# Linear attention taken four heads at a time, with its instructions regrouped and half of its weight-sum transfers moved

## The chip, the cores and the metric

The kernel runs on one core of a Trainium2 chip. The metric is the device time of one launch, in microseconds (us). The kernel before takes 1200.89 us, the median of three runs (1200.57 to 1201.19).

## What is computed

One transformer-like layer on x (1024 tokens by 1024 channels), in float32. Three mixers share one input projection, then an output projection and a squared-ReLU MLP of width 4096 follow:

```
h = rms_norm(x, ln1_g);  z = h @ w_in
y_conv = short_conv(...)            # 256 channels
y_diff = diff_attention(...)        # 4 heads, q and k 2 x 64, v 128
y_gla  = gla(g_q, g_k, g_v, g_g, ...)   # 4 heads of 64, chunks of 64 tokens
x = x + concat(y_conv, y_diff, y_gla) @ w_out
x = x + square(relu(rms_norm(x, ln2_g) @ w_mlp1)) @ w_mlp2
```

The change is in `gla`, the gated linear attention. For each chunk of 64 tokens and each head it needs three products (scores of the chunk with itself, those scores times v, and the queries times the state carried from the chunks before):

```
att     = where(causal, einsum('bcthd,bcshd->bchts', q_in, k_in), 0)
o_intra = einsum('bchts,bcshe->bcthe', att, vf)
o_inter = einsum('bcthd,bchde->bcthe', q_in, s_prev)
o = rms_norm(o_intra + o_inter, norm_g) * silu(g_out)
```

## The kernel before

**Products.** Large products keep float32 precision by splitting each operand into a high and a low part; `mm3` (L157 to L160) issues three matmuls for each piece: L158, L159, L160. A projection tile (`gemm_b`, L180) is 128 tokens by 256 columns of `w_in`: 8 pieces of the 1024 channels, so 24 matmuls, into one of three PSUM banks named `ps_mm`. The small products of linear attention are single float32 matmuls; each appears in the trace as two passes, each with a weight load (PEld) and a matmul (PE).

**Linear attention.** The four heads lie in two pairs (`pr`); within a pair, head `hh` has partitions 0 to 63 or 64 to 127 (`po = hh * 64`). `eb` holds the queries, `enb` the keys, `S` the states, `gv` the values. The loop before (L520 to L524) runs over 16 steps g: a token tile tt of 128 tokens and one hh, so two heads in each step. `gla_scores(g)` (L494) makes two matmuls that read 64 partitions and write 128 columns, then masks them into one of four tiles `att` (L496, VectorE). `gla_out(g)` adds up, for either pair, a full matmul `att` by `gv` (L506) and two matmuls of 64 partitions by 64 columns, `eb` by `S`, one for each chunk of the tile (L509), in one PSUM bank `ps_tr`; ScalarE copies the result out (L513) and squares it (L514), VectorE sums the squares (L515).

**What runs between.** The generator `steps01` yields one projection tile at each `next`: 8 tiles of q (`qraw`), 8 of k (`kraw`) and 8 of v (`dv`) for heads 0 and 1 of differential attention. The loop takes one tile in each step; the last 7 tiles run after it. Loads of `w_in` (L146, in `load_w`) go by SP's queue into two stage buffers `wst`; ScalarE and VectorE split them (L138, L139), one projection ahead of their use.

**Weight sums.** The MLP needs sums of blocks of its weights. They are made by transfers in device memory: POOL's queue copies a block (L118) and later adds another to it (L121). There are 64 such transfers of 1 MB each, in a fixed order: `w1s` (32), then `w2s` (32). `next_sum(when)` (L130 to L134) issues the next one: a tiny POOL copy `paced` (L132) waits for `when`, the transfer stands behind it in POOL's queue. In the kernel before they are paced by: 4 tiles of `kE`, 4 of `eb`, the 16 steps of the linear attention loop (on `ssg`), 8 query tiles in each of four attention heads (32, on `sso`), and 8 steps of the MLP.

A scheduler orders the instructions of each engine; the program sets what each depends on. Attention (`attention(0)` to `attention(3)`) follows the loop, with the other projections between. At the end of attention 3 the mixed outputs are stored to device memory (`ydram`, L218) and read back (L706) for the output projection; ScalarE and VectorE split them into `yTh` and `yTl`.

The order of a loop step, and its PSUM bank:

```
gla_scores(0)
for g in range(2 * NT):
    if g + 1 < 2 * NT:
        gla_scores(g + 1)
    next(steps01)
    gla_out(g)
```

Of the kernel before, what the change touches and what calls it, by code (L numbers as in the profile page):

```python
# [9 lines left out]
F32 = mybir.dt.float32  # L10
# [3 lines left out]
AF = mybir.ActivationFunctionType  # L14
ALU = mybir.AluOpType
AX = mybir.AxisListType
# [3 lines left out]
P = 128  # L20
T = 1024
D = 1024
NT = T // P
# [13 lines left out]
def hybrid_block(ctx, tc, x, ln1_g, w_in, conv_w, q_norm_g, k_norm_g, diff_lambda, diff_subln_g,  # L37
                 gla_alpha_w, gla_alpha_b, gla_norm_g, w_out, ln2_g, w_mlp1, w_mlp2, out):
    nc = tc.nc
# [19 lines left out]
    def ps_s():  # L59
        return psum.tile([P, 512], F32, name="ps_s", tag="s", bufs=2)  # L60

    def ps_tr():
        return psum.tile([P, 512], F32, name="ps_tr", tag="tr", bufs=2)
# [66 lines left out]
    def next_sum(when):  # L130

        g = nc.gpsimd.tensor_copy(paced, when)  # L132
        with tc.issue_after(g.ins):
            next(sum_steps)  # L134
# [6 lines left out]
    def load_w(w, c0, ncol):  # L141
        wb = []
        for kh in range(2):
            st = stage().rearrange("p (c n) -> p c n", c=4)
            wk = w[kh * 512:(kh + 1) * 512, :].rearrange("(c p) n -> p c n", p=P)
            nc.sync.dma_start(st, wk[:, :, c0:c0 + 256])  # L146
            hi = wpool.tile([P, 4, 272], F32R, name="whi", tag="hi", bufs=4)
            lo = wpool.tile([P, 4, 272], F32R, name="wlo", tag="lo", bufs=4)
            split(hi[:, :, 0:256], lo[:, :, 0:256], st)
            if ncol > 256:  # L150
                sx = c1.tile([P, 4, ncol - 256], F32, name="sx", tag="sx", bufs=2)
                nc.sync.dma_start(sx, wk[:, :, c0 + 256:c0 + ncol])
                split(hi[:, :, 256:ncol], lo[:, :, 256:ncol], sx)
            wb.append((hi, lo))
        return wb
# [10 lines left out]
    def gemm_a(wb, m0, mcols, act, th):  # L166
        ps = ps_mm()
        for kc in range(KC):
            hi, lo = wb[kc // 4]
            ah, al = act[th][kc // 4]  # L170
            mm3(ps[0:mcols, :], hi[:, kc % 4, m0:m0 + mcols], lo[:, kc % 4, m0:m0 + mcols],
                ah[:, kc % 4, :], al[:, kc % 4, :], kc == 0, kc == KC - 1)
        return ps

    def gemm_b(wb, act, tt, ncol=256, ks=tuple(range(KC))):
        ps = ps_mm()
        th, o = tt // 4, (tt % 4) * P
        for kc in ks:
            hi, lo = wb[kc // 4]
            ah, al = act[th][kc // 4]  # L180
            mm3(ps[:, 0:ncol], ah[:, kc % 4, o:o + P], al[:, kc % 4, o:o + P],
                hi[:, kc % 4, 0:ncol], lo[:, kc % 4, 0:ncol], kc == ks[0], kc == ks[-1])
        return ps
# [28 lines left out]
    gp = gla_cm.__enter__()  # L212

    def g4(nm):
        return gp.tile([P, 1024], F32, name=nm, tag="g4", bufs=8)
# [7 lines left out]
    def c4(nm):  # L223
        return cv.tile([P, T], F32, name=nm, tag="cz", bufs=3)
# [63 lines left out]
    gv = r1.tile([P, NT, 256], F32, name="gv", tag="v")  # L288
# [75 lines left out]
    eb = [g4("eb") for _ in range(2)]  # L364
    enb = [g4("enb") for _ in range(2)]
    dec = [c1.tile([P, 16], F32, name=f"dec{p}") for p in range(2)]
    for pr in range(2):
        for th in range(2):
            ps = ps_s()
            for i in range(4):  # L370
                tt = th * 4 + i
                c0 = (tt % 4) * 256 + pr * P
# [8 lines left out]
    for pr in range(2):  # L381
        for th in range(2):
            ts_ = slice(th * 512, (th + 1) * 512)
            ps = gemm_a(wb, pr * P, P, hT, th)
# [11 lines left out]
    S = [g4("S") for _ in range(2)]  # L396
    for pr in range(2):
        nc.gpsimd.memset(S[pr][:, 0:64], 0.0)
        kv = [ps_s(), ps_s()]
        for c in range(15):  # L400
            tt, po = c // 2, (c % 2) * 64
            for hh in range(2):
# [3 lines left out]
                                 start=True, stop=True)  # L406
# [9 lines left out]
    for pr in range(2):  # L416
        for th in range(2):
            ts_ = slice(th * 512, (th + 1) * 512)
            ps = gemm_a(wb, pr * P, P, hT, th)
# [8 lines left out]
        nc.vector.tensor_tensor(gv_, gv_, sg, op=ALU.mult)  # L428


    def qk_steps(c0, nm, got):
        wb = load_w(w_in, c0, 256)
        raw = r1.tile([P, NT, 256], F32, name=nm, tag="raw")
        got.append(raw)
        ss = stat.tile([P, 32], F32, name="ssqk", tag="ssqk", bufs=4)
        for tt in range(NT):
            ps = gemm_b(wb, hT, tt)
            nc.scalar.copy(raw[:, tt, :], ps[:, 0:256])
            sq = r1.tile([P, 256], F32, name="sqa", tag="sqa")
            nc.scalar.activation(sq, ps[:, 0:256], AF.Square)  # L440
            nc.vector.tensor_reduce(ss[:, tt * 4:tt * 4 + 4], sq.rearrange("p (h e) -> p h e", e=64),
                                    axis=AX.X, op=ALU.add)
            if tt % 4 == 3:
                th = tt // 4
                mq = stat.tile([P, 16], F32, name="mq", tag="mq")
                nc.vector.tensor_scalar(mq, ss[:, th * 16:th * 16 + 16], 1.0 / 64, EPS, op0=ALU.mult, op1=ALU.add)
                rq = rstd_of(mq, 16, "q16")
                for i in range(4):
                    rv = raw[:, th * 4 + i, :].rearrange("p (a e) -> p a e", e=64)
                    nc.vector.tensor_tensor(rv, rv, rq[:, i * 4:i * 4 + 4].unsqueeze(2).broadcast_to([P, 4, 64]),  # L450
                                            op=ALU.mult)
            yield

    def v_steps(pair, got):
        wb = load_w(w_in, C_DV + pair * 256, 256)
        v = r1.tile([P, NT, 256], F32, name="dv", tag="v")
        got.append(v)
        for tt in range(NT):
            ps = gemm_b(wb, hT, tt)
            nc.scalar.copy(v[:, tt, :], ps[:, 0:256])  # L460
            yield

    def run(steps):
        for _ in steps:
            pass

    def qk_raw(c0, nm):
        got = []
        run(qk_steps(c0, nm, got))
        return got[0]  # L470

    def v_proj(pair):
        got = []
        run(v_steps(pair, got))
        return got[0]

    qkv01 = []
    steps01 = chain(qk_steps(C_DQ, "qraw", qkv01), qk_steps(C_DK, "kraw", qkv01), v_steps(0, qkv01))


    attb = [gp.tile([P, 2, P], F32, name=f"att{i}") for i in range(4)]
    for a in attb:
        nc.gpsimd.memset(a, 0.0)
    og = [c4("og") for _ in range(2)]
    ssg = c1.tile([P, 32], F32, name="ssg")
    maskv = cum.bitcast(I32).unsqueeze(1).broadcast_to([P, 2, P])
    next(steps01)

    def gla_scores(g):
        tt, hh = g // 2, g % 2  # L490
        tsl, po = slice(tt * P, (tt + 1) * P), hh * 64
        ps = ps_s()
        for pr in range(2):
            nc.tensor.matmul(ps[:, pr * P:(pr + 1) * P], enb[pr][po:po + 64, tsl], eb[pr][po:po + 64, tsl],  # L494
                             start=True, stop=True)
        nc.vector.copy_predicated(attb[g % 4], maskv, ps[:, 0:256].rearrange("p (h t) -> p h t", h=2))  # L496

    def gla_out(g):
        tt, hh = g // 2, g % 2
        po, att = hh * 64, attb[g % 4]  # L500
        ov = og[tt // 4][:, (tt % 4) * 256:(tt % 4) * 256 + 256].rearrange("p (r h e) -> p r h e", r=2, h=2)
        po_ = ps_tr()
        for pr in range(2):
            os_ = slice(pr * 64, (pr + 1) * 64)
            h0 = pr * P + hh * 64
            nc.tensor.matmul(po_[:, os_], att[:, pr, :], gv[:, tt, h0:h0 + 64], start=True, stop=False)  # L506
            for i in range(2):
                c = tt * 2 + i
                nc.tensor.matmul(po_[i * 64:(i + 1) * 64, os_],  # L509
                                 eb[pr][po:po + 64, c * 64:(c + 1) * 64],  # L510
                                 S[pr][po:po + 64, c * 64:(c + 1) * 64], start=False, stop=True)
        sq = gp.tile([P, P], F32, name="sqg", tag="sqg", bufs=2)
        nc.scalar.copy(ov[:, :, hh, :], po_[:, 0:P].rearrange("p (r e) -> p r e", r=2))  # L513
        nc.scalar.activation(sq, po_[:, 0:P], AF.Square)  # L514
        nc.vector.tensor_reduce(ssg[:, tt * 4:tt * 4 + 4].rearrange("p (r h) -> p r h", r=2)[:, :, hh],  # L515
                                sq.rearrange("p (r e) -> p r e", r=2), axis=AX.X, op=ALU.add)
        next_sum(ssg[0:1, tt * 4 + hh:tt * 4 + hh + 1])

    gla_scores(0)
    for g in range(2 * NT):  # L520
        if g + 1 < 2 * NT:
            gla_scores(g + 1)
        next(steps01)
        gla_out(g)  # L524
    for th in range(2):
        mg = stat.tile([P, 16], F32, name="mg", tag="mg")
        nc.vector.tensor_scalar(mg, ssg[:, th * 16:th * 16 + 16], 1.0 / 64, EPS, op0=ALU.mult, op1=ALU.add)
# [1 line left out]
        ov = og[th].rearrange("p (a e) -> p a e", e=64)  # L529
# [132 lines left out]
    zs = r1.tile([P, 2, T], F32, name="zs", tag="v")  # L662
    wb = load_w(w_in, C_U, 256)
    for m in range(2):
        for th in range(2):
            ps = gemm_a(wb, m * P, P, hT, th)
            nc.scalar.copy(zs[:, m, th * 512:(th + 1) * 512], ps)
    attention(3, (q23, k23, v23), bias)
    wb = load_w(w_in, C_C, 256)
    accs = []  # L670
    for m in range(2):
        for th in range(2):
            ps = gemm_a(wb, m * P, P, hT, th)
# [36 lines left out]
    for m in range(2):  # L710
        for th in range(2):
            ps = gemm_a(wb, m * P, P, hT, th)
# [80 lines left out]
    for tt, nh in [(t, h) for h in range(2) for t in range(NB)] + [(t, h) for t in range(NB, NT) for h in range(2)]:  # L793
        if tt not in x1:
            x1_tile(tt)
        ps = gemm_o(tt, nh)
# [3 lines left out]
        if waiting:  # L800
            t = waiting.pop(0)
# [250 lines left out]
```

## Time and profile before

| | |
|---|---|
| median of three runs | 1200.89 us (1200.57 to 1201.19) |
| the profiled execution, its own time | 1198.36 us |
| its span, first to last instruction | 1196.7 us |
| TensorE (PE) matmul busy | 1175.5 us, 98% |
| PE weight loads (PEld) busy | 994.8 us, 83% |
| VectorE (DVE) / ScalarE (ACT) / POOL busy | 743.8 / 518.5 / 73.2 us |
| mean granted TensorE clock | 0.997 of full |

Times in the trace are us from the span's start. PE and PEld are two views of one engine: a weight load may run beside an earlier matmul, and the end of a matmul is modelled, so the starts of successive weight loads tell the pace. The linear attention loop lies at about 139 to 212 us, attention 0 to 3 at about 236 to 472 us, the output projection from there to about 570 us, then the MLP. In a row, `<-` behind a bracketed number names what ended the engine's idle time before the instruction.

### The profile page before, as it was taken

To read this page: it belongs to the slowest core of one execution; us is meant where nothing else is said; L and a number is where in the kernel's file an instruction comes from. 1 tells how busy PE (TensorE), PEld (TensorE's weight loads), DVE (VectorE), ACT (ScalarE), POOL (GpSimd) and SP (SyncE) were. 2 spreads that over 40 slices of the span, in tenths; PEclk is the share of its full clock that TensorE was granted. 3 is DMA by queue.
4 is the path that set the end of the run, shared out by engine and by line. 5 is a ranking of instruction groups with operands and counts; after the bars stand their busy time and mean duration, and the time that the engine had idled before them with its cause. 6 is when DMAs were issued, how large, how long until landed. Compare 5 with 4: busy or idle time off the path is not lost.

```text
span 1196.7 us, 16779 instructions
## 1 busy us (share of the span) xinstructions
PE 1175.5 (98%) x6423; PEld 994.8 (83%) x6423; DVE 743.8 (62%) x1334; ACT 518.5 (43%) x976; POOL 73.2 (6%) x159
## 2 busy tenths in 40 slices
PE   8999999999999998999999999999999999999998
PEld 6997899989997886788788888888888888888887
DVE  6535654386849695546877677667674654565553
ACT  5542133366647653423653434343433333333332
POOL 3001121010201111000000000000000000000000
PEclk9999999999999999999999999999999999999999
DMA  6124699758744979741566776777799985666000
GB/s 193 58 71 176 201 215 270 183 168 180 214 122 98 230 211 213 233 143 53 165 196 206 242 233 215 203 220 229 242 359 391 386 300 208 214 213 208 1 36 35
DMA packets 117074, 231.35 MB, mean 193 GB/s; under 512 B 7651, under 2 KB 49665, under 8 KB 113666
## 3 DMA queue, kind: packets, MB, share of 16 engines
q1 hardware_dynamic: 100290, 160.00, 39.3%
q0 software_dynamic: 14976, 67.14, 23.7%
q10 hardware_dynamic: 1728, 3.15, 0.7%
q8 instruction: 50, 0.82, 0.3%
q14 instruction: 30, 0.25, 0.1%
HBM read 189.37 MB, written 108.00 MB: 248 GB/s over the span
## 4 chain that ended last, share of the span: by engine, by line
PE 85%; DVE 5%; DMA 4%; ACT 4%; issue 1%; SPq 0%; POOL 0%; ACTq 0%; DVEq 0%; POOLq 0%
PE pso L158 8%; PE pso L160 8%; PE pso L159 8%; PE psp L159 8%; PE psp L160 8%; PE psp L158 8%; PE ps_mm L158 8%; PE ps_mm L160 7%; PE ps_mm L159 7%; PE ps_av L628 3%; PE ps_s L598 1%; PE ps_tr L620 1%; DMA wst<-in_w_out_dram 1%; PE ps_s L599 1%; DMA ydram<-yt 1%; DMA wst<-ydram 1%
## 5 line engine op out<-in xcount | busy, mean ns | idle before, releaser
L158 PE MATMUL pso<-o2l,o2h 128*128 128x512 f32 x448 | 174.3, 389 | 0.0
L159 PE MATMUL pso<-o2h 128*128 128x512 f32 x448 | 174.3, 389 | 0.0
L160 PE MATMUL pso<-o2h,o2l 128*128 128x512 f32 x448 | 174.3, 389 | 0.0
L139 DVE TENSOR_TENSOR o2l<-f,o2h 128x1024 fp32r<-128x1024 f32 x56 | 68.5, 1224 | 139.9 <-ACT o2h L138 139.9
L158 PE MATMUL ps_mm<-wlo,hTh 128*128 128x256 f32 (+1 forms) x512 | 148.2, 290 | 3.2 <-DVE wlo L139 2.5
L160 PE MATMUL ps_mm<-whi,hTl 128*128 128x256 f32 (+1 forms) x512 | 146.3, 286 | 0.0
L159 PE MATMUL ps_mm<-whi,hTh 128*128 128x256 f32 (+1 forms) x512 | 146.1, 285 | 0.0
L138 ACT CAST o2h<-f 128x1024 fp32r<-128x1024 f32 x56 | 59.0, 1053 | 191.7 <-PE pso L159 186.4
L158 PEld LDWEIGHTS ps_mm<-wlo,hTh 128*128 128x128 f32 x512 | 97.2, 190 | 7.3 <-ACT hTh L203 3.4
L160 PEld LDWEIGHTS pso<-o2h,o2l 128*128 128x128 f32 x448 | 84.1, 188 | 17.5
L159 PEld LDWEIGHTS pso<-o2h 128*128 128x128 f32 x448 | 84.1, 188 | 17.5
L158 PEld LDWEIGHTS pso<-o2l,o2h 128*128 128x128 f32 x448 | 84.1, 188 | 17.3
L160 PEld LDWEIGHTS ps_mm<-whi,hTl 128*128 128x128 f32 x512 | 97.3, 190 | 1.2 <-issue 0.7
L159 PEld LDWEIGHTS ps_mm<-whi,hTh 128*128 128x128 f32 x512 | 97.0, 189 | 1.2 <-issue 0.7
L138 ACT CAST w1h<-wst 128x1024 fp32r<-128x1024 f32 x56 | 59.1, 1055 | 85.6 <-PE psp L159 77.0
L886 DVE TENSOR_TENSOR s<-psp,s 128x512 f32<-128x512 f32 x96 | 64.6, 688 | 44.9 <-PE psp L160 40.3
L139 DVE TENSOR_TENSOR w1l<-wst,w1h 128x1024 fp32r<-128x1024 f32 x56 | 68.4, 1221 | 21.6 <-ACT w1h L138 21.5
L158 PE MATMUL ps_mm<-hTl,whi 128*128 128x512 f32 x160 | 65.2, 407 | 5.8 <-DVE yt L714 5.8
L139 DVE TENSOR_TENSOR o2l<-w,o2h 128x1024 fp32r<-128x1024 f32 x56 | 68.2, 1218 | 0.0
L159 PE MATMUL ps_mm<-hTh,whi 128*128 128x512 f32 x160 | 65.5, 409 | 0.0
L160 PE MATMUL ps_mm<-hTh,wlo 128*128 128x512 f32 x160 | 64.6, 404 | 0.0
L138 ACT CAST o2h<-w 128x1024 fp32r<-128x1024 f32 x56 | 58.9, 1052 | 2.8 <-PE psp L159 2.8
(309 smaller groups left out, 2457.5 us busy)
## 6 DMA issues: line engine op xcount, KB each, us to landing
f<-fdram SPq DMA_DIRECT2D x28, 1024.0 KB, 8.7
w1s<-in_w_mlp_dram POOLq DMA_DIRECT2D x24, 1024.0 KB, 9.5
w2s<-in_w_mlp_dram POOLq DMA_DIRECT2D x24, 1024.0 KB, 11.9
wst<-w1s SPq DMA_DIRECT2D x32, 512.0 KB, 4.2
w<-w2s SPq DMA_DIRECT2D x16, 1024.0 KB, 7.2
wst<-in_w_in_dram SPq DMA_DIRECT2D x26, 512.0 KB, 5.1
wst<-in_w_mlp_dram SPq DMA_DIRECT2D x24, 512.0 KB, 4.1
fdram<-s SPq DMA_DIRECT2D x48, 256.0 KB, 2.3
```

What stands on the lines that cost most here:

```text
L138: nc.scalar.copy(hi, src)
L139: return nc.vector.tensor_tensor(lo, src, hi.bitcast(F32), op=ALU.subtract)
L158: nc.tensor.matmul(ps, lh, rl, start=first, stop=False)
L159: nc.tensor.matmul(ps, lh, rh, start=False, stop=False)
L160: return nc.tensor.matmul(ps, ll, rh, start=False, stop=last)
L598: nc.tensor.matmul(ps[:, 0:w], qi, kll[c][:, j * 512:j * 512 + w], start=True, stop=False)
L599: nc.tensor.matmul(ps[:, 0:w], qi, khh[c][:, j * 512:j * 512 + w], start=False, stop=True)
L620: nc.tensor.transpose(tp[:, b * P:(b + 1) * P], pc[0][:, (b0 + b) * P:(b0 + b + 1) * P], ident)
L628: nc.tensor.matmul(av[:, 0:P], aT[:, b * P:(b + 1) * P], v[:, kb, hh * P:hh * P + P], start=(kb == 0), stop=(kb == i))
L886: nc.vector.tensor_tensor(dst, a_, b_, op=op)
```

## The change

The linear attention loop now runs over 8 token tiles, all four heads in each, with two projection tiles taken between. Matmuls that read partitions 0 to 63 and those that read 64 to 127 alternate and write different PSUM banks (`ps[0]`, `ps[1]`; `po_[0]`, `po_[1]`). The full matmuls of the tile (four) stand together, then the eight of 64 by 64, then the four score matmuls of the next tile. The loop issues 8 weight-sum transfers instead of 16; the other 8 are issued in projections after it: 2 in the v projection of heads 2 and 3, 4 in their q and k projections, 2 in the first convolution projection. The 64 transfers and their order stay.

```diff
-    def qk_steps(c0, nm, got):
+    def qk_steps(c0, nm, got, sums=False):
...
+                if sums:
+                    next_sum(rq[0:1, 0:1])
             yield
 
-    def v_steps(pair, got):
+    def v_steps(pair, got, sums=False):
...
+            if sums and tt % 4 == 3:
+                next_sum(v[0:1, tt, 0:1])
             yield
...
-        run(qk_steps(c0, nm, got))
+        run(qk_steps(c0, nm, got, True))
...
-        run(v_steps(pair, got))
+        run(v_steps(pair, got, True))
...
+    def gla_scores(tt):
+        tsl = slice(tt * P, (tt + 1) * P)
+        ps = [ps_s(), ps_s()]
         for pr in range(2):
+            for hh in range(2):
+                po = hh * 64
+                nc.tensor.matmul(ps[hh][:, pr * P:(pr + 1) * P], enb[pr][po:po + 64, tsl], eb[pr][po:po + 64, tsl],
+                                 start=True, stop=True)
+        for hh in range(2):
+            nc.vector.copy_predicated(attb[tt % 2 * 2 + hh], maskv, ps[hh][:, 0:256].rearrange("p (h t) -> p h t", h=2))
+
+    def gla_out(tt):
+        po_ = [ps_tr(), ps_tr()]
+        for hh in range(2):
+            for pr in range(2):
+                h0 = pr * P + hh * 64
+                nc.tensor.matmul(po_[hh][:, pr * 64:(pr + 1) * 64], attb[tt % 2 * 2 + hh][:, pr, :], gv[:, tt, h0:h0 + 64],
+                                 start=pr == 0, stop=False)
         for pr in range(2):
             for i in range(2):
                 c = tt * 2 + i
+                for hh in range(2):
+                    po = hh * 64
+                    nc.tensor.matmul(po_[hh][i * 64:(i + 1) * 64, pr * 64:(pr + 1) * 64],
+                                     eb[pr][po:po + 64, c * 64:(c + 1) * 64],
+                                     S[pr][po:po + 64, c * 64:(c + 1) * 64], start=False, stop=pr == 1)
...
+        next_sum(ssg[0:1, tt * 4:tt * 4 + 1])
...
     gla_scores(0)
-    for g in range(2 * NT):
-        if g + 1 < 2 * NT:
-            gla_scores(g + 1)
-        next(steps01)
-        gla_out(g)
+    for tt in range(NT):
+        for _ in range(2):
+            next(steps01)
+        gla_out(tt)
+        if tt + 1 < NT:
+            gla_scores(tt + 1)
...
             nc.scalar.copy(zs[:, m, th * 512:(th + 1) * 512], ps)
+        next_sum(zs[0:1, m, 512:513])
```

**TensorE, one step of the loop before** (g = 2; `att2` and the banks `ps_tr`, `ps_s` as named above, the numbers are those of buffers; the row behind is the next projection tile's first):

```order
L506 MATMUL ps_tr_1604<-gv_254,att2_1408 128x64
L509 MATMUL ps_tr_1604<-S_1164,eb_970 64x64 x2
L506 MATMUL ps_tr_1604<-gv_254,att2_1408 128x64
L509 MATMUL ps_tr_1604<-S_1165,eb_971 64x64 x2
L494 MATMUL ps_s_1617<-eb_970,enb_972 128x128
L494 MATMUL ps_s_1617<-eb_971,enb_973 128x128
L158 MATMUL ps_mm_1621<-wlo_1420,hTh_118 128x256
```

**TensorE, the tile tt = 1 now**, which is what the steps g = 2 and 3 were (the full matmuls are L510, two on each bank; those of 64 by 64 are L517; the scores L500):

```order
L510 MATMUL ps_tr_1631<-gv_254,att2_1408 128x64 x2
L510 MATMUL ps_tr_1632<-gv_254,att3_1409 128x64 x2
L517 MATMUL ps_tr_1631<-S_1164,eb_970 64x64
L517 MATMUL ps_tr_1632<-S_1164,eb_970 64x64
L517 MATMUL ps_tr_1631<-S_1164,eb_970 64x64
L517 MATMUL ps_tr_1632<-S_1164,eb_970 64x64
...
L500 MATMUL ps_s_1655<-eb_970,enb_972 128x128
L500 MATMUL ps_s_1656<-eb_970,enb_972 128x128
L500 MATMUL ps_s_1655<-eb_971,enb_973 128x128
L500 MATMUL ps_s_1656<-eb_971,enb_973 128x128
```

A step went from full to 64 by 64, back to full, to 64 by 64, and to the scores before the projection; a tile now goes through each form once, and successive matmuls of 64 partitions stand in different banks. Behind the loop, the order of the matmuls is as before.

**POOL's queue at the loop's end, before** (`w1s_100` is a sum that receives its second block, `w1s_101` the next one's copy; IOTA belongs to attention 0):

```order
L132 COPY paced<-ssg 1x1
L121 DMA w1s_100<-in_w_mlp_dram 128x2048
L547 IOTA bias 128x1024
L132 COPY paced<-ssg 1x1
L118 DMA w1s_101<-w1s_99 16x16384
L132 COPY paced<-ssg 1x1
L118 DMA w1s_101<-w1s_99 16x16384
```

and now:

```order
L132 COPY paced<-ssg 1x1
L121 DMA w1s_100<-in_w_mlp_dram 128x2048
L132 COPY paced<-sso 1x1
L118 DMA w1s_101<-w1s_99 16x16384
L132 COPY paced<-sso 1x1
L118 DMA w1s_101<-w1s_99 16x16384
```

The copies into `w1s_101` and all behind them now wait for `sso`, the query tiles of attention 0, instead of the loop; the order of the transfers is the same. SP's queue is unchanged row by row.

## Rows read from the trace of the kernel before

**Rows 1.** The page, part 1 (busy us, share, instructions) and part 4 (chain).

```profile
PE 1175.5 (98%) x6423; PEld 994.8 (83%) x6423; DVE 743.8 (62%) x1334; ACT 518.5 (43%) x976; POOL 73.2 (6%) x159
...
PE 85%; DVE 5%; DMA 4%; ACT 4%; issue 1%; SPq 0%; POOL 0%; ACTq 0%; DVEq 0%; POOLq 0%
```

**Rows 2.** Windows: busy us (instructions) by engine, granted clock, DMA share, GB/s.

```profile
139.57:211.59 72.02, 72.02 (x608) 65.63 (x607) 34.67 (x95) 22.18 (x73) 14.77 (x31) 1.00 0.93 222
...
405.00:427.00 22.00, 21.66 (x110) 16.63 (x109) 17.11 (x45) 14.78 (x33) 1.80 (x4) 1.00 1.01 219
427.00:443.00 16.00, 16.00 (x95) 13.49 (x94) 15.53 (x47) 9.70 (x29) 2.87 (x6) 1.00 0.80 263
443.00:472.50 29.50, 29.50 (x162) 24.00 (x160) 18.22 (x40) 10.81 (x27) 4.83 (x8) 1.00 1.01 202
...
478.37:484.00 5.63, 5.63 (x14) 4.43 (x15) 5.45 (x9) 4.00 (x7) 0.00 (x0) 0.51 0.58 181
```

**Rows 3.** Timeline of weight loads: start us, us covered, load, xcount; first, second, last step.

```profile
139.57 0.52 PEld L494 LDWEIGHTS ps_s<-eb,enb 64*128 64x128 f32 x4
140.20 0.19 PEld L158 LDWEIGHTS ps_mm<-wlo,hTh 128*128 128x128 f32 x1
...
144.57 0.19 PEld L160 LDWEIGHTS ps_mm<-whi,hTl 128*128 128x128 f32 x1
144.69 0.31 PEld L506 LDWEIGHTS ps_tr<-gv,att 128*128 128x128 f32 x2
145.07 0.19 PEld L509 LDWEIGHTS ps_tr<-S,eb 64*64 64x64 f32 x4
145.33 0.30 PEld L506 LDWEIGHTS ps_tr<-gv,att 128*128 128x128 f32 x2
145.69 0.20 PEld L509 LDWEIGHTS ps_tr<-S,eb 64*64 64x64 f32 x4
145.96 0.52 PEld L494 LDWEIGHTS ps_s<-eb,enb 64*128 64x128 f32 x4
146.59 0.19 PEld L158 LDWEIGHTS ps_mm<-wlo,hTh 128*128 128x128 f32 x1
...
210.33 0.31 PEld L506 LDWEIGHTS ps_tr<-gv,att 128*128 128x128 f32 x2
...
211.59 0.31 PEld L535 LDWEIGHTS ps_tr<-ident,og 128*128 128x128 f32 x3
```

**Rows 4.** Groups of the stretch 139.5 to 211.7 us: busy us, mean ns, idle before.

```profile
L506 PEld LDWEIGHTS ps_tr<-gv,att 128*128 128x128 f32 x64 | 9.7, 189 | 1.1
...
L494 PEld LDWEIGHTS ps_s<-eb,enb 64*128 64x128 f32 x64 | 8.3, 186 | 1.2
...
L509 PEld LDWEIGHTS ps_tr<-S,eb 64*64 64x64 f32 x128 | 6.2, 131 | 2.2
...
L513 ACT COPY og<-ps_tr 128x128 f32<-128x128 f32 x15 | 4.0, 265 | 9.1 <-PE ps_tr L509 9.1
```

**Rows 5.** Timeline of weight loads at the state products of one pair (L403).

```profile
131.29 1.42 PEld L403 LDWEIGHTS ps_s<-gv,kE 64*64 64x64 f32 x60 [0.25 <-issue]
```

**Rows 6.** Timeline of ScalarE: two splits' casts in the loop, then the stores behind it.

```profile
170.07 1.05 ACT L138 CAST whi<-wst 128x1024 fp32r<-128x1024 f32 x1
...
205.12 1.05 ACT L138 CAST whi<-wst 128x1024 fp32r<-128x1024 f32 x1 [1.80 <-PE ps_mm L160]
...
226.80 0.69 ACT L537 ACTIVATE yt<-ps_tr,cols 128x512 f32<-128x512 f32 x1 [2.64 <-DMA ydram<-yt]
```

**Rows 7.** Loads of `w_in` (L146) issued at 165 to 212 us, their landing.

```profile
DMA to landing us min/median/max: 17.7/19.1/25.9
```

**Rows 8.** Timeline of PE: the idle times at 228 and 478 us.

```profile
228.31 0.39 PE L158 MATMUL ps_mm<-wlo,hTh 128*128 128x256 f32 x1 [0.51 <-ACT dv L460]
...
478.37 0.80 PE L158 MATMUL ps_mm<-hTl,whi 128*128 128x512 f32 x1 [5.82 <-DVE yt L714]
```

**Rows 9.** Timeline of ScalarE: the wait for the outputs read back.

```profile
472.99 0.62 ACT L138 CAST yTh<-wst 128x512 fp32r<-128x512 f32 x1 [8.77 <-DMA wst<-ydram]
```

**Rows 10.** Uses of `w1s`: transfers, first and last start us.

```profile
L832 SPq DMA_DIRECT2D wst<-w1s x32: 359/371/386, 507.3 to 857.4; - x32
...
L121 POOL DMA_DIRECT2D w1s<-in_w_mlp_dram x16: 812/827/857, 144.0 to 279.4; - x16
```

More of the change, by code (lines that the diff above doesn't have):

```diff
@@ L487, in hybrid_block @@
     next(steps01)
[L489 to L492, printed above, removed]
+    def gla_scores(tt):
+        tsl = slice(tt * P, (tt + 1) * P)
+        ps = [ps_s(), ps_s()]
         for pr in range(2):
-            nc.tensor.matmul(ps[:, pr * P:(pr + 1) * P], enb[pr][po:po + 64, tsl], eb[pr][po:po + 64, tsl],
-                             start=True, stop=True)
-        nc.vector.copy_predicated(attb[g % 4], maskv, ps[:, 0:256].rearrange("p (h t) -> p h t", h=2))
@@ L498, in gla_out @@
[L498 to L502, printed above, removed]
+            for hh in range(2):
[4 more added lines that the diff above has]
+            nc.vector.copy_predicated(attb[tt % 2 * 2 + hh], maskv, ps[hh][:, 0:256].rearrange("p (h t) -> p h t", h=2))
@@ L503, in gla_out @@
+    def gla_out(tt):
[5 more added lines that the diff above has]
+                                 start=pr == 0, stop=False)
         for pr in range(2):
-            os_ = slice(pr * 64, (pr + 1) * 64)
-            h0 = pr * P + hh * 64
-            nc.tensor.matmul(po_[:, os_], att[:, pr, :], gv[:, tt, h0:h0 + 64], start=True, stop=False)
@@ L507, in gla_out @@
             for i in range(2):
                 c = tt * 2 + i
[L509 to L514, printed above, removed]
@@ L515, in gla_out @@
-        nc.vector.tensor_reduce(ssg[:, tt * 4:tt * 4 + 4].rearrange("p (r h) -> p r h", r=2)[:, :, hh],
-                                sq.rearrange("p (r e) -> p r e", r=2), axis=AX.X, op=ALU.add)
-        next_sum(ssg[0:1, tt * 4 + hh:tt * 4 + hh + 1])
-    gla_scores(0)
-    for g in range(2 * NT):
-        if g + 1 < 2 * NT:
-            gla_scores(g + 1)
-        next(steps01)
-        gla_out(g)
+                for hh in range(2):
[3 more added lines that the diff above has]
+                                     S[pr][po:po + 64, c * 64:(c + 1) * 64], start=False, stop=pr == 1)
@@ new lines, in gla_out @@
+        ov = og[tt // 4][:, (tt % 4) * 256:(tt % 4) * 256 + 256].rearrange("p (r h e) -> p r h e", r=2, h=2)
+        for hh in range(2):
+            sq = gp.tile([P, P], F32, name="sqg", tag="sqg", bufs=2)
+            nc.scalar.copy(ov[:, :, hh, :], po_[hh][:, 0:P].rearrange("p (r e) -> p r e", r=2))
+            nc.scalar.activation(sq, po_[hh][:, 0:P], AF.Square)
+            nc.vector.tensor_reduce(ssg[:, tt * 4:tt * 4 + 4].rearrange("p (r h) -> p r h", r=2)[:, :, hh],
+                                    sq.rearrange("p (r e) -> p r e", r=2), axis=AX.X, op=ALU.add)
```

## The prediction

> **What bounds the kernel now.** I read the page first: TensorE is busy 98% of the span and carries 85% of the chain that ended last [rows 1]. Then the windows: in the linear attention loop, 139.57 to 211.59 us, PE is busy for all of its 72.02 us, while VectorE needs 34.67 and ScalarE 22.18 [rows 2]. So a microsecond less of TensorE work there is a microsecond less of time, unless something behind it becomes late. The DMA share in the loop is 0.93: the memory queues are nearly full, but nothing waits for them there.
>
> Then the timeline of weight loads, since their starts give TensorE's pace [rows 3]. Between two projection matmuls it is 0.12 us (144.57 to 144.69). A loop step's small products start at 144.69 and the projection is back at 146.59: 1.90 us. Its parts, start to start:
> - full loads (L506), two: 144.69 to 145.07, 0.38 us
> - 64 by 64 (L509), four: 145.07 to 145.33, 0.26 us
> - both again: 145.33 to 145.96, 0.63 us
> - scores (L494), four: 145.96 to 146.59, 0.63 us
>
> The reader is to see two things. A pair of full loads covers 0.31 us, so the second starts 0.31 - 0.19 = 0.12 us after the first; yet the next form comes 0.26 us after that second load. Changing the form costs about 0.14 us more than a load in the same form. And the four 64 by 64 loads, each 131 ns [rows 4], cover only 0.19 us: the two of different columns run side by side, a second pass follows 0.06 us behind. The score loads, 186 ns each [rows 4], cover 0.52 us with four, so they follow each other at (0.52 - 0.19) / 3 = 0.11 us: they all stand on the same 64 partitions and take turns.
>
> **The change, part by part.** *Removed:* the small products of the loop before take 2 x 0.63 us (the first two score groups, such as 139.57 to 140.20), 14 steps of 1.90 us and 2 last steps of 1.26 us (such as 210.33 to 211.59) [rows 3]: 1.3 + 26.6 + 2.5 = 30.4 us.
>
> *Added:* per tile of four heads, no matmul more or less.
> - Eight full loads together: the first two and the change of form 0.38 us, six more at 0.11: 1.04 us.
> - Sixteen 64 by 64 loads, four on each quarter of the array. If the quarters run side by side, each has two passes more than in the row, at 0.06: 0.26 + 0.12 = 0.38 us.
> - Eight score loads, four on either half of the partitions. If the halves run side by side: 0.63 + 0.01 = 0.64 us.
>
> That is 2.06 us a tile, 1.42 without scores. Total: the first scores 1.3 us (still in two groups, as the order shows no alternation there), 8 x 1.42 = 11.4, 7 x 0.64 = 4.5: 17.1 us. **The loop gains 30.4 - 17.1 = 13.3 us.** The full matmuls and the changes of form are paid from rows; the running side by side of different partitions is the open term. The nearest row is the 60 loads of 64 by 64 for the state products: in pairs they would take 30 x 0.06 = 1.8 us, they took 1.42 [rows 5]; the order puts most matmuls of one half before those of the other. So halves do overlap where the order lets them. Bounds of the gain: with no overlap of halves, the quarters go in pairs (0.26 + 3 x 0.12 = 0.62 us) and the scores in turn (0.63 + 4 x 0.11 = 1.07): 2.73 a tile, 1.3 + 8 x 1.66 + 7 x 1.07 = 22.1 us in all, a gain of 8.3. With full overlap, 13.3. I take 13.3, since the row lies between and the new order alternates at every matmul.
>
> The Trainium skill, "TensorEngine Tiling (Array Packing)", section Key Properties, says that a change of tiling mode drains the engine and that tiles otherwise run independently; the trace agrees on the first with its 0.14 us a change, and by that rule alone, seven of ten changes saved in each of 8 tiles, an estimate would be 56 x 0.14 = 7.8 us.
>
> *New waits in the loop.* Each tile's masks, squares and copies now follow two projection tiles (2 x 24 x 0.12 = 5.7 us) instead of one; ScalarE and VectorE have well under half of the stretch to do [rows 2], and both `ps_tr` banks and both `ps_s` banks have those 5.7 us to come free. I cost this at nothing; without that cover a tile would wait for a copy out of PSUM, 0.27 us [rows 4], 2 us over 8 tiles. The w_in loads for the next projection but one are issued when the stage is split (170.07) and needed 35 us later (205.12) [rows 6]; they land in 17.7 to 25.9 us [rows 7]. The shorter loop leaves 8 steps of projection less 13.3 / 2: some 28 us, still above the worst row, and with half of the sum transfers in the way they land sooner.
>
> *Behind the loop.* The sums there held up a store: ScalarE waited for `ydram` (2.64 us at 226.80 [rows 6]) and PE lost 0.51 us to it [rows 8]. With 8 transfers fewer I take that 0.5 us as gained; bounds 0 and 0.5.
>
> *The moved sums.* Eight POOL copies and eight issues change their place in POOL's queue; behind them there stand only other sums, and SP's queue is untouched. `w1s` is first read at 507.3 us, its last sum was issued at 279.4 [rows 10] and comes some 40 us later now: 180 us to spare. By the end of attention 3, 56 transfers are issued as before, and its own eight are the same ones. But from the start of attention 2 to there go 18 transfers instead of 16, where the DMA share is 1.01 at 405 to 427 and 443 to 472 us [rows 2]. The stretch between them, 0.80, can take the two more (0.2 x 16 = 3.2 us free). Cost: none, with an upper bound among the rivals.
>
> **The sum:** 13.3 + 0.5 = 13.8 us. The profiled execution took 1198.36 us, so 1184.6; the median of the runs is 2.5 us above it, 1200.89, and the measured time should be **1187.1 us**.
>
> **The rivals.**
> *The halves do not overlap, or in part.* For: the score loads in the trace never alternate halves, so nothing shows it for that shape. Against: the 1.42 us of [rows 5]. Gain 8.3 + 0.5 at the least: 1192.1 us; half way, 1189.6. The Trainium skill, "TensorE: Matmul & The Clock Gate", Part 3, holds that matmuls start and end in program order, without reordering. Applied to passes, a matmul's second pass would hold back the next matmul's first, and the gain would fall between these two; the four L509 loads that cover 0.19 us speak against it here.
>
> *The stall at 472 us moves.* ScalarE waits 8.77 us for the outputs read back [rows 9], PE then 5.82 us [rows 8]; after that idle time the clock is granted at 0.51, the 1.2 GHz level, for 5.63 us [rows 2], half of which, 2.8 us, is lost. The change alters neither, but it shifts when they fall. Without the drop: 1184.3 us; with a drop of twice the length, 1189.9.
>
> *Slower.* At that same wait the two transfers more that cross the full queues could delay the read-back. PE idles one to one with it there. From 13.8 us of delay on, the gain is gone; the worst landing of a load in a crowded stretch was 25.9 us [rows 7], against a wait of 8.77 here: 17.1 us more, and the time would be 1187.1 + 17.1 = 1204.2 us. Against: the free 3.2 us before it, and the same eight transfers beside it.
>
> *Nothing changes* only if that delay comes to 11.4 to 16.2 us.
>
> **How the numbers follow.** The forecast has 0.68, the halves 0.14, the stall 0.11, slower 0.03, no change 0.03, and 0.01 for the rest. About 0.2% (2.4 us) is what a measurement here tells from no change. The first three all lie beyond it on the fast side: faster 0.94, same 0.03, slower 0.03. The range reaches from the stall without its drop and a read-back 1 us sooner, 1183.3, to the lower bound of the overlap, 1192.1, with 0.3 for the runs' own spread: 1183.0 to 1192.4 us.
>
> **What the profile will show.** Right: the loop lasts about 58.7 us instead of 72.0, PE busy throughout; a tile's small products take 2.06 us from the first L510 load to the projection; sixteen L517 loads cover about 0.3 us and eight L500 loads about 0.53; no idle PE at 228 less 13 us; the same 5.8 us stall after attention 3. Wrong: L500 loads at 0.11 us in one row after another (2.5 to 2.7 us a tile); PE idle in the loop on ScalarE or VectorE; a ScalarE wait on `ydram` well above 8.77 us.

## The result and the profile after

The changed kernel takes 1186.20 us (median of 4 runs, 1185.81 to 1186.57) against 1200.73 us (4 runs, 1199.83 to 1201.19) for the kernel before: ratio 0.9878, 95% interval 0.9866 to 0.9889, so 14.5 us faster. Its profiled execution took 1186.37 us, with a span of 1184.7.

The page of the changed kernel, parts 1 and 4, answers to [rows 1]:

```profile
PE 1161.1 (98%) x6423; PEld 986.0 (83%) x6423; DVE 743.8 (63%) x1334; ACT 517.8 (44%) x976; POOL 75.0 (6%) x159
...
PE 88%; DVE 5%; ACT 3%; DMA 2%; issue 1%; SPq 0%; POOL 0%; ACTq 0%; DVEq 0%; POOLq 0%
```

TensorE has the same 6423 matmuls and is busy 14.4 us less; the span is 12.0 us shorter. Its windows, columns as in [rows 2], show the loop and the stretch behind the wait at 460 us:

```profile
140.41:199.33 58.92, 58.92 (x608) 56.63 (x607) 33.95 (x94) 20.91 (x71) 8.07 (x15) 1.00 0.73 146
...
466.00:472.00 6.00, 5.99 (x14) 4.73 (x15) 5.55 (x9) 4.09 (x7) 0.00 (x0) 0.50 0.62 193
```

The loop lasts 58.92 us instead of 72.02, PE is busy in all of it, and the DMA share fell from 0.93 to 0.73. One tile in the timeline of weight loads, as in [rows 3]:

```profile
151.26 0.19 PEld L160 LDWEIGHTS ps_mm<-whi,hTl 128*128 128x128 f32 x1
151.38 0.98 PEld L510 LDWEIGHTS ps_tr<-gv,att 128*128 128x128 f32 x8
152.42 0.32 PEld L517 LDWEIGHTS ps_tr<-S,eb 64*64 64x64 f32 x16
152.81 0.52 PEld L500 LDWEIGHTS ps_s<-eb,enb 64*128 64x128 f32 x8
153.46 0.19 PEld L158 LDWEIGHTS ps_mm<-wlo,hTh 128*128 128x128 f32 x1
```

From 151.38 to 153.46 are 2.08 us for four heads, where the loop before took 2 x 1.90 = 3.80. Over the loop the small products fell from 30.4 to 17.3 us (two first scores of 0.64, seven tiles of 2.08, a last one of 1.44): 13.1 us. The weight loads issued in the loop, in answer to [rows 7]:

```profile
L146 SPq DMA_DIRECT2D wst<-in_w_in_dram x4: 367/368/368, 165.3 to 198.3; - x4
...
DMA to landing us min/median/max: 6.5/6.9/7.1
```

They land in 7 us instead of 18 to 26. The waits of [rows 8] and [rows 9], in the timelines of PE and ScalarE:

```profile
466.01 0.80 PE L158 MATMUL ps_mm<-hTl,whi 128*128 128x512 f32 x1 [5.89 <-DVE yt L726]
```

```profile
460.63 0.62 ACT L138 CAST yTh<-wst 128x512 fp32r<-128x512 f32 x1 [8.84 <-DMA wst<-ydram]
```

The wait of 0.51 us behind the loop is gone; the one after attention 3 stayed (5.89 us against 5.82), with the clock at 0.50, the 1.2 GHz level, behind it.

Where the span's 12.0 us come from, by the same matmuls in the two traces: at the start the changed kernel's profiled execution is 0.84 us late (its clock was at half from 7.8 to 18.1 us; that of before was not), at the start of the attention it is 12.7 us early, so 13.6 us came from the loop (13.1) and the wait behind it (0.5); 0.7 us are given back in pieces of 0.1 to 0.4 us from the attention to the output projection. The median of before was 2.5 us above its own profiled execution, that of the changed kernel is not, so the medians differ by more than the spans.

### The profile page after: what moved, and what is told of

Read it like the earlier page. It is cut to its first block, busy times and chain, and to the rows that moved or that the text cites. A ratio compares the mean times of both kernels' runs of the same rounds, so it can differ in the third digit from the quotient of the medians.

```text
span 1184.7 us, 16782 instructions
## 1 busy us (share of the span) xinstructions
PE 1161.1 (98%) x6423; PEld 986.0 (83%) x6423; DVE 743.8 (63%) x1334; ACT 517.8 (44%) x976; POOL 75.0 (6%) x159
## 4 chain that ended last, share of the span: by engine, by line
PE 88%; DVE 5%; ACT 3%; DMA 2%; issue 1%; SPq 0%; POOL 0%; ACTq 0%; DVEq 0%; POOLq 0%
PE ps_mm L158 9%; PE pso L159 9%; PE pso L158 9%; PE pso L160 9%; PE ps_mm L160 8%; PE psp L160 8%; PE ps_mm L159 8%; PE psp L159 8%; PE psp L158 8%; PE ps_av L639 3%; PE ps_s L609 2%; PE ps_tr L631 1%; PE ps_s L610 1%; DMA wst<-ydram 1%; PE ps_tr L510 1%
## 5 line engine op out<-in xcount | busy, mean ns | idle before, releaser
L159 PEld LDWEIGHTS pso<-o2h 128*128 128x128 f32 x448 | 84.1, 188 | 17.3
```

Of the source, the lines that this page charges most:

```text
L159: nc.tensor.matmul(ps, lh, rh, start=False, stop=False)
```

## The experiments

Two questions: what in the new loop saves TensorE's time, and what the moved sums are for. Times below stand against the kernel before on the same chip: 1201.19 us (23 runs) for the first four kernels, 1200.91 (9) for e5, e6, e8 and e9, 1200.23 (11) for e10 to e12, 1200.10 (9) for e13.

### e1_sums_only and e2_loop_only: either half of the change

The loop of before with its sums halved, and the new loop with all 16:

```diff
-        next_sum(ssg[0:1, tt * 4 + hh:tt * 4 + hh + 1])
+        if hh == 1:
+            next_sum(ssg[0:1, tt * 4:tt * 4 + 1])
```

```diff
-        next_sum(ssg[0:1, tt * 4:tt * 4 + 1])
+        for hh in range(2):
+            next_sum(ssg[0:1, tt * 4 + hh:tt * 4 + hh + 1])
```

(e1 also has the change's eight issues behind the loop, e2 has none of them.)

> The loop before, with only the eight weight-sum transfers moved. Theory (the gain is TensorE's, in the loop's small products; the moved transfers give back only the 0.5 us for which PE waited behind the store): 0 to 0.6 us faster than before, 1200.1 to 1200.7 us; a loop step's small products still take 1.90 us. Rival (the crowded memory queues held the loop back): several us faster, up to 13.

> The new loop with all sixteen transfers left in it, two a tile. Theory: a tile's small products take 2.08 us as in the changed kernel, the loop is 13.1 us shorter; PE's wait behind the store comes back with 0.5 us or somewhat more, since the same 16 transfers meet in a shorter loop: 1186.2 to 1188.0 us. Rival (the shorter loop needs the transfers out of its way, since the loads of w_in then land too late): PE idle in the loop or right behind it, 1190 us and more.

Measured: e1 1199.34 us (12 runs), ratio 0.9983 (0.9975 to 0.9992), 1.9 us gained, more than the 0 to 0.6 expected and far from its rival's several us. e2 1206.69 us (6 runs), ratio 1.0038 (1.0026 to 1.0051): **the new loop alone is 5.5 us slower than before.** The profile of e2 says why; its loop in the windows, then a load's landing, then ScalarE and PE in the timelines:

```profile
160.00:200.00 40.00, 40.00 (x425) 38.58 (x424) 24.09 (x62) 14.75 (x49) 11.13 (x21) 1.00 1.07 272
...
218.50:224.00 5.50, 5.50 (x27) 5.50 (x26) 2.56 (x11) 1.59 (x3) 1.88 (x4) 0.50 0.82 215
```

```profile
L146 SPq DMA_DIRECT2D wst<-in_w_in_dram x4: 367/368/368, 165.8 to 218.5; - x4
...
  ACT whi L138: 19.5, 1
...
DMA to landing us min/median/max: 3.8/20.6/48.3
```

```profile
216.14 1.04 ACT L138 CAST whi<-wst 128x1024 fp32r<-128x1024 f32 x1 [19.55 <-DMA wst<-in_w_in_dram]
```

```profile
218.21 1.54 PE L546 MATMUL ps_tr<-ident,og 128*128 128x128 f32 x6 [17.45 <-ACT sqg L524]
```

A load of `w_in` issued at 167.8 us lands 48.3 us later, at 216.1. ScalarE stands at its cast for 19.55 us, and behind the cast in its order wait the copies and squares that empty the last tile's banks: PE idles for 17.45 us and comes back at half clock for 5.9 us more, of which half is lost. That is more than the 13.1 us which the loop had saved. The sums of e2 that add a block (L121) land one every 5.2 us or so in a row, the four that copy from `w1s` itself (L118) one every 3.2: for the sixteen an estimate of 12 x 5.2 + 4 x 3.2, some 75 us of transfer, in a loop of 59.

### e4_full_first and e9_full_first_sums: the order of the forms, with and without the sums

The loop of before, but the two full matmuls ahead of the four of 64 by 64, so three changes of form a step instead of five; e9 is e4 with the change's moved sums.

```diff
+            nc.tensor.matmul(po_[:, os_], att[:, pr, :], gv[:, tt, h0:h0 + 64], start=pr == 0, stop=False)
+        for pr in range(2):
+            os_ = slice(pr * 64, (pr + 1) * 64)
             for i in range(2):
```

> The loop before with one edit: both full matmuls of a step before its four of 64 by 64, so three changes of form a step instead of five; no halves alternate. Theory (a change costs some 0.14 us beyond a load in the same form): a step's small products take 1.90 - 0.29 = 1.61 us, 16 steps save 4.6 us: 1196.1 us. Rival (a change of form costs nothing, all of the gain is overlap of halves): 1.90 us and 1200.7.

> The loop of the kernel before with the full products ahead of the 64-column ones (1.62 us a step instead of 1.90, as measured), and with half of its weight sums moved to the later projections as in the changed kernel. Theory that the shorter steps were lost before only because 16 sums held the DMA queues and a weight load landed 44 us late: the load now lands in time, TensorE does not wait at the loop's end, and the 16 steps of 0.285 us come through: 1199.3 less 4.6, so 1194.5 to 1195.5. Rival, that the faster loop loses its gain in any case (a wait elsewhere takes it): 1198.5 to 1201.

e4: 1201.65 us (12 runs, 1198.34 to 1211.05, a spread of 12.7 us where the changed kernel's is 0.8), ratio 1.0014 (0.9992 to 1.0035), no gain; e9: 1194.07 us (5 runs), ratio 0.9946 (0.9934 to 0.9959). A step of e4 in the timeline of weight loads:

```profile
159.05 0.53 PEld L506 LDWEIGHTS ps_tr<-gv,att 128*128 128x128 f32 x4
159.65 0.31 PEld L511 LDWEIGHTS ps_tr<-S,eb 64*64 64x64 f32 x8
160.03 0.52 PEld L494 LDWEIGHTS ps_s<-eb,enb 64*128 64x128 f32 x4
160.67 0.19 PEld L158 LDWEIGHTS ps_mm<-wlo,hTh 128*128 128x128 f32 x1
```

1.62 us instead of 1.90: two changes of form less, 0.28 us, so 0.14 us a change. In e4 that was lost to the same cause as in e2, here in the timeline of ScalarE (its profiled execution took 1205.69 us, 4.0 above the median):

```profile
215.64 1.04 ACT L138 CAST whi<-wst 128x1024 fp32r<-128x1024 f32 x1 [10.58 <-DMA wst<-in_w_in_dram]
```

The load took 43.9 us, PE waited 8.62. e9 has the same 1.62 us a step, its loads land in 5.6 to 6.8 us, PE does not wait, and the time lies 5.3 us under e1 (4.4 by the two ratios) where the steps alone give 30.4 - 25.9 = 4.5.

### e3_halves_in_turn and e8_same_half: what the two halves of the partitions do

e3 is the changed kernel with the loops over `hh` outside, so all matmuls of one half come before those of the other. e8 groups as many heads, in the same forms, but two token tiles' heads of one half.

```diff
-        for pr in range(2):
-            for hh in range(2):
+        for hh in range(2):
+            for pr in range(2):
```

```diff
+    def gla_scores(g):
+        u, hh = g // 2, g % 2
+        po = hh * 64
...
+            for j in range(2):
+                tsl = slice((2 * u + j) * P, (2 * u + j + 1) * P)
+                nc.tensor.matmul(ps[j][:, pr * P:(pr + 1) * P], enb[pr][po:po + 64, tsl], eb[pr][po:po + 64, tsl],
```

> The changed kernel, but all matmuls of one partition half before those of the other, so that no two successive ones alternate; banks, forms and their three changes a tile stay. Theory (the halves run side by side only where they alternate): a tile's small products take 2.4 to 2.7 us instead of 2.08, the time is 2.5 to 5 us above the changed kernel, 1188.7 to 1191.2. Rival (the gain is all in the fewer changes of form): 2.08 us and 1186.2.

> The changed kernel with as large a group, as many changes of form and the same products in it, but the four heads of a group are two token tiles' heads of one half of the partitions instead of one tile's heads of both halves. Theory that both halves standing together is what lets the quarter products and the scores overlap: a group takes 2 x 1.62 us (the two one-half blocks measured with the full products first) less three changes of form of 0.14 us, about 2.8 us instead of 2.08, and the time is 1191 to 1192. Rival, that only the size of the group and the changes of form count: 2.08 us a group and 1186.2.

e3: 1185.77 us (4 runs), ratio 0.9870 (0.9857 to 0.9883), the changed kernel's time; e8: 1192.53 us (5 runs), ratio 0.9934 (0.9922 to 0.9947). A tile of e3 and a group of e8:

```profile
152.03 0.98 PEld L510 LDWEIGHTS ps_tr<-gv,att 128*128 128x128 f32 x8
153.07 0.34 PEld L517 LDWEIGHTS ps_tr<-S,eb 64*64 64x64 f32 x16
153.48 0.53 PEld L500 LDWEIGHTS ps_s<-eb,enb 64*128 64x128 f32 x8
154.13 0.19 PEld L158 LDWEIGHTS ps_mm<-wlo,hTh 128*128 128x128 f32 x1
```

```profile
160.12 0.98 PEld L513 LDWEIGHTS ps_tr<-gv,att 128*128 128x128 f32 x8
161.17 0.59 PEld L519 LDWEIGHTS ps_tr<-S,eb 64*64 64x64 f32 x16
161.83 0.96 PEld L501 LDWEIGHTS ps_s<-eb,enb 64*128 64x128 f32 x8
162.91 0.19 PEld L158 LDWEIGHTS ps_mm<-wlo,hTh 128*128 128x128 f32 x1
```

In e8 the sixteen quarter loads cover 0.59 us and the eight score loads 0.96, against 0.32 and 0.52 in the changed kernel: on one half the score loads take turns, and the quarter loads (those of 64 by 64) run two at a time; on two halves they all run side by side. In e3, where the four 64 by 64 matmuls and the two score matmuls of one half stand ahead of those of the other, the loads still cover 0.34 and 0.53. So the halves must stand in the same group; they need not alternate. The time of e3 is also what its rival forecast, that the gain is all in the fewer changes of form; e8, with the same changes of form, rules that out.

This closes the account of a tile of four heads: 3.80 us before; 3.23 with two steps of e4 (four changes of form less); 2.79 in e8 (three more); 2.08 with both halves in the group. Over the whole loop: 30.4, 25.9, 22.5 and 17.3 us, that is 7.9 us from changes of form and 5.2 from the halves.

### e5_two_tiles: a larger group

Two token tiles in a group, after four projection steps.

```diff
-    for tt in range(NT):
-        for _ in range(2):
+    for u in range(NT // 2):
+        for _ in range(4):
```

> The changed kernel with two token tiles in a group: eight heads' small products stand together after four projection steps, so the loop has 4 groups instead of 8 and half as many changes of form (three fewer in each of four places, some 13 in all). Theory that a change of form costs about 0.14 us: the small products fall from 17.3 to about 15.5 us and the time from 1186.2 to about 1184.4. Rival, that the gain came from both halves standing together alone and changes of form cost little: no change, 1186.2. Second rival: with both tiles' casts and squares behind one group the PSUM buffers come free late and TensorE waits in each group, 1187 or more.

1186.10 us (4 runs), ratio 0.9879 (0.9865 to 0.9892): no gain, though the small products fell by somewhat more than expected, 17.3 to 15.1 us (3.66 us a group of eight heads). The timelines of PE and of ScalarE show where it went:

```profile
214.48 0.39 PE L158 MATMUL ps_mm<-wlo,hTh 128*128 128x256 f32 x1 [1.62 <-ACT dv L462]
```

```profile
211.12 0.69 ACT L556 ACTIVATE yt<-ps_tr,cols 128x512 f32<-128x512 f32 x1 [7.26 <-DMA ydram<-yt]
```

The last two sums begin 1.3 us apart just as the loop ends, the first two stores behind it take 11.4 and 12.1 us, ScalarE waits for their buffer and PE 1.62 us for ScalarE.

### e6_sums_late and e10_sums_spread: the wait after attention 3

The last four sums of attention 3 in the MLP instead: e6 in its steps 0 to 3, e10 in steps 2 to 5, a second sum beside the one of each step.

```diff
-            next_sum(ss[0:1, i:i + 1])
+            if h < 3 or i < 4:
+                next_sum(ss[0:1, i:i + 1])
...
+        if 2 <= q < 6:
+            next_sum(f[1][2][0:1, 0:1])
```

> The changed kernel with the last four weight-sum transfers of attention 3 begun in the MLP's first four steps instead. In the loop kernel with all 16 sums left in it a load that stood behind sums in the DMA queues landed 48 us late and TensorE waited 17.5 us. Theory that the 5.9 us wait at 460 us (and the 2.8 us that the half clock behind it costs) has the same cause, sums in flight beside the read-back of the attention's rows: the store and the read-back land in about 2 us each instead of 9 and 10, the wait goes, and the time falls to 1178 to 1182. Rival, that this wait is the length of the chain of store, read-back and casts by itself: it stays near 5.9 us, and the time stays at 1186. Second rival: the four sums are then late for the MLP, and the time rises.

> The changed kernel with the last four weight sums of attention 3 begun one each in the MLP's steps 2 to 5, where the step that held them in pairs (step 0) had made weight loads late and cost 1.2 us. Theory that the earlier attempt kept 3 us of a possible 4.2 because of that pair at 592 us: the wait at 460 us stays near 0.6 us, no wait of TensorE at 632 us, 1182 to 1183. Rival, that sums anywhere in the MLP delay its weight loads: 1183.5 to 1185.

e6: 1183.67 us (4 runs), ratio 0.9854 (0.9838 to 0.9869), less than expected. e10: 1182.43 us (4 runs), ratio 0.9847 (0.9834 to 0.9860). The read-back of `ydram` in e6, then PE:

```profile
DMA to landing us min/median/max: 3.2/3.7/4.2
```

```profile
460.85 0.50 PE L158 MATMUL ps_mm<-hTl,whi 128*128 128x512 f32 x1 [0.62 <-DVE yt L727]
...
475.03 0.50 PE L158 MATMUL ps_mm<-wol,yTh 128*128 128x512 f32 x1 [2.35 <-DVE wol L139]
...
633.35 0.47 PE L158 MATMUL psp<-H4l,w1h 128*128 128x512 f32 x1 [0.96 <-ACT s L892]
```

The read-back lands in 4 us instead of 9 to 10, and the wait of 5.89 us becomes 0.62: it was the sums in flight, as in the loop. But the next thing is late in its place, the first `w_out` load (2.35 us), with half clock for 3.4 us behind it; and the pair of sums in MLP step 0 takes 14 and 18 us and costs 1.2 us there. In e10, without that pair, this second loss is gone, the `w_out` waits are 1.41 and 1.0 us, and the clock stays at full behind it.

### e11_both_early, e12_twelve and e13_even_pace: number or spacing

e12: the changed kernel with 12 sums in the loop. e11: e5 and e10 together, the loop's 8 sums as 3, 3, 2 and 0 behind its four groups. e13: the same, but a sum after every second projection step:

```diff
-            for k in range((1, 2)[j] if u < 2 else u == 2):
-                next_sum(ssg[0:1, tt * 4 + k:tt * 4 + k + 1])
...
+            n = 1 + 4 * u + k
+            if k % 2 == 0:
+                next_sum(qkv01[n // 8][0:1, n % 8, 0:1])
```

> Two token tiles in a group, with the loop's 8 sums in its first three groups and none in the last, and the last four sums of attention 3 one each in the MLP's steps 2 to 5. Theory that the two-tile group's 2.2 us were lost to a 1.6 us wait at the loop's end because the stores of its rows stood behind sums in flight (11 and 12 us to land): these stores land in 2 to 5 us, the wait goes, and the time is that of the other kernel with the late sums less 2 us, 1180 to 1181. Rival, that the wait comes with the group's size (casts and squares of two tiles behind one another): 1.6 us at the loop's end again, 1182 to 1183.

> The changed kernel with 12 sums in the loop instead of 8 (two in every second tile; the four of the q and k projections stay in the loop). In the loop kernel with 16 the sums landed one every 5.2 us, so 16 need 83 us and 12 need 62 in a loop of 58.7 us, and a weight load issued meanwhile landed only when the row of sums was nearly empty. Theory that what counts is whether the sums fit into the loop: about 60 us of work for 59, the load lands in 10 to 30 us, little or no wait at the loop's end, 1186 to 1189. Rival, that any sum above eight costs its 5.2 us at the loop's end: some 10 us and half clock behind it, 1195 or more.

> The kernel of the run before last (two token tiles in a group, four sums late) with the loop's 8 sums begun one after every second projection step, some 7.5 us apart and the last some 12 us ahead of the loop's end, instead of two or three at once behind a group. Three at once had let a weight load land 35 us late. Theory that the bunching did that, since a sum alone lands in 8 us and the next begins after it: the weight loads land in 5 to 10 us, the stores behind the loop in 2 to 5 us, TensorE waits under 0.5 us at the loop's end, and the 2.2 us of the two-tile group come through: 1180 to 1181. Rival, that the two-tile group brings its own wait at the loop's end, whatever the sums do: over 1 us of idle there, 1182 to 1184.

e12: 1185.88 us (4 runs), ratio 0.9876 (0.9862 to 0.9890), no loss. e11: 1181.48 us (6 runs), but from 1177.41 to 1187.57, ratio 0.9847 (0.9822 to 0.9872): inconclusive as a time. Its profile, though, has what the expectation did not foresee, in the timeline of ScalarE and PE's wait behind it (6.65 us):

```profile
199.06 1.04 ACT L138 CAST whi<-wst 128x1024 fp32r<-128x1024 f32 x1 [7.34 <-DMA wst<-in_w_in_dram]
```

**e13: 1177.39 us** (5 runs, 1176.73 to 1178.30), ratio 0.9812 (0.9799 to 0.9826), 3 us under the expected 1180 to 1181 and, between the medians, 8.8 under the changed kernel (7.9 by the two ratios). Its windows at the loop and where the wait after attention 3 was, and PE there:

```profile
140.65:197.20 56.55, 56.55 (x609) 55.52 (x608) 33.41 (x94) 20.71 (x67) 7.88 (x14) 1.00 0.82 167
...
457.00:463.00 6.00, 5.20 (x23) 3.93 (x22) 5.76 (x10) 3.58 (x7) 0.00 (x0) 1.00 0.58 175
```

```profile
458.52 0.50 PE L158 MATMUL ps_mm<-hTl,whi 128*128 128x512 f32 x1 [0.80 <-DVE yt L737]
```

PE has no idle time of over 0.4 us at the loop's end, and after 0.80 us of idle at 458 the clock stays at 1.00. Against e10 the small products are the expected 2.2 us shorter, and the profiled spans lie 3.3 us apart (1179.9 and 1176.6), 0.6 of it ahead of the loop; the medians lie 5.0 apart (4.2 by the ratios), and why they do stays open. The sums began less evenly than meant, 5 to 11 us apart and the last at 197.7 us, as the loop ended; the stores behind it land in 6.2 and 6.7 us, not in 2 to 5, and that was enough. The kernels with the `w_in` load issued inside the loop, side by side, from their traces:

| kernel | sums in the loop, how begun | that load lands after | PE idle at the loop's end |
|---|---|---|---|
| before | 16, one per 4.7 us | 25.9 us | none |
| e4 | 16, one per 4.45 us | 43.9 us | 8.62 us |
| e2 | 16, two per 7.75 us | 48.3 us | 17.45 us |
| e12 | 12, three per 15.5 us | 17.8 us | none |
| e11 | 8, three at once per 15 us | 35.1 us | 6.65 us |
| e5 | 8, two at once per 15 us | 5.0 us | none (1.62 us at 214) |
| changed | 8, one per 7.75 us | 6.5 us | none |
| e13 | 8, one per 5 to 11 us | 4.9 us | none |

An adding sum alone lands in about 8 us, and a row of them one every 5.2 us. Begun faster than that, they form a row, and the load lands when that row has almost emptied (e2: 216.1 us, with a sum landing at 215.9; e11: 199.0 and 199.4); in the kernel before and in e12 two sums were still under way then. Even the kernel before begins them slightly faster, and their landing there grows from 8.4 to 12.8 us along the row. That e5 begins its sums in pairs and the load still lands in 5.0 us may be due to the row it meets: one sum was under way when it was issued, in e11 two, and three more began within 6 us. Why the load does not get its share beside them stays open.

## Why the prediction was right, point by point

**The loop's small products.** Forecast 30.4 to 17.1 us, measured 17.3; a tile 2.08 us against 2.06, the L517 loads 0.32 us against 0.3, the L500 loads 0.52 against 0.53, the loop 58.92 us against 58.7. The step held, both parts of it: 0.14 us a change of form, and the halves side by side. The lower bound without the second, a gain of 8.3 us, is what e8 measures: 7.9. Its reason was wrong in one place: full overlap was taken "since the new order alternates at every matmul", and e3 has it without alternating, at 2.10 us a tile. The rival that the halves do not overlap fell. The Trainium skill, "TensorEngine Tiling (Array Packing)", section Key Properties, has changes of mode drain the engine and tiles run independently. The trace agrees: the estimate of 7.8 us by the first alone stands beside 7.9 measured, and the second is the other 5.2. The Trainium skill, "TensorE: Matmul & The Clock Gate", Part 3, has matmuls start and end in program order. The trace of e3 does not bear this out: from its first L517 load to its first L500 load are 0.41 us, in the changed kernel 0.39, and if the second half could begin only behind the start of the first half's last matmul, two passes of 0.06 us later, e3 would take an estimated 0.51.

**New waits in the loop.** Forecast none, and there are none. In part this was luck, since the argument was too weak: the loads had "some 28 us, still above the worst row" of 25.9, as if a shorter loop left the landing alone. e2 shows the landing at 48.3 us when the loop shortens with its 16 sums. Only the clause behind it, that half of the transfers are out of the way, made the step come true.

**The moved sums.** Their own cost was forecast at nothing, and the medians show none: e1 gains 1.9 us. The profile of e1 puts 0.8 of these at the loop's end; where the rest lies stays open. That execution is the slowest of e1's twelve (1201.74 us): after attention 3 PE waits 6.8 us in it instead of 5.8, and 2.6 us more for the first `w_out` loads, so a cost of this part in some executions is not ruled out. In the changed kernel's profile these waits are 5.9 and 0.3. What the sum missed is that this part carries the other: the new loop without it costs 5.5 us, with it gains, 20.5 us apart. It did not change the forecast, since both were made at once.

**Behind the loop.** The 0.5 us wait went, and with fewer sums about, as taken, the stores that it hung on land sooner: in 9.0 and 10.5 us instead of 10.4 and 13.1. In e1, where the sums alone moved, they land in 7.4 and 7.8, and PE does not wait there. ScalarE has two waits for them, of which [rows 6] shows the second; before, the first was

```profile
223.47 0.69 ACT L537 ACTIVATE yt<-ps_tr,cols 128x512 f32<-128x512 f32 x1 [4.64 <-DMA ydram<-yt]
```

and now they are

```profile
210.51 0.69 ACT L548 ACTIVATE yt<-ps_tr,cols 128x512 f32<-128x512 f32 x1 [3.94 <-DMA ydram<-yt]
212.56 0.69 ACT L548 ACTIVATE yt<-ps_tr,cols 128x512 f32<-128x512 f32 x1 [1.36 <-DMA ydram<-yt]
```

Together they fell from 7.3 to 5.3 us, and they no longer reach PE.

**The stall after attention 3.** It stayed, as the forecast had it, at 5.89 us and with the same length of half clock (6.8 us in either trace); the rival that it moves fell, and so did the slower one (the read-back waits 8.84 us against 8.77). What the text took for a given length, e6 and e10 show to be the same contention of sums, and removable.

**The sum.** 13.8 us forecast, 13.6 found in the trace up to the attention, 14.5 between the medians (13.3 to 16.1 by the interval), 12.0 between the two profiled executions; the differences are the clock at the start of one of them, the small losses named above, and how far each profiled execution lies from its median.

## What to carry to other kernels

Put small matmuls of one form together, and those of both partition halves into the same group; the price of a change of form is read from the start times of weight loads. Before shortening a compute-bound stretch, divide the transfers in it by the new length: background transfers that just fitted can make a load late, and the time comes back as a wait on an engine that seemed unconcerned. Space background transfers so that each lands before the next begins, and keep them away from stores that are read back at once.

## What was not expected of the hardware

A change between matmul forms cost 0.14 us in e4, 0.15 in e8 (2 x 1.62 - 2.79 over three) and 0.17 in e5 (2 x 2.08 - 3.66 over three). Matmuls of 64 partitions in the two halves overlap even with four of one half queued ahead of the other's, at 2.10 against 2.08 us a tile. And the landing of a plain load among the sums depends on how they are begun more than on their number: 4.9 us among eight begun one at a time (e13), 35.1 among eight begun in threes (e11), 25.9 among sixteen begun one at a time.
